# Which 48 expert tiles get their first product early: tiles 0 to 47, or 48 spread evenly over all 128

## The chip, the core and the metric

The kernel runs on one core of a Trainium2 chip. The metric is the device time of one execution in microseconds (us); for the kernel before it is the median of three runs. The profile is of one execution more, and its times count from the start of its span.

## What is computed

The reference is a decoder block: two gated token mixers, a memory attention, and an expert layer. The change lies in the expert layer, whose core is this:

```python
def chunk(args):                      # 128 tokens
    hc, ic, gc = args                 # states, 128 expert numbers and 128 gates per token
    a = jnp.einsum('cd,ced->ce', hc, u[ic])
    a = jax.nn.gelu(a, approximate=False) * gc.astype(hc.dtype)
    return jnp.einsum('ce,ced->cd', a, v[ic])
```

There are 1024 tokens of width 1024 and 16384 experts. Each token uses 128 of the experts, each a row of `u` and a row of `v`.

## The kernel before

The tokens are worked in two halves of four blocks of 128. The first half **gathers** its expert rows: GpSimd issues an indirect DMA for each expert slot (L1035 for `u`, L1051 for `v`, 512 of each, 0.5 MB apiece), and VectorE multiplies the rows (L1038 for `u`, L1057 for `v`). These steps are spread over the program by a pace: each piece of matmul work ticks a clock by its cost (`self.pace.tick`), and the next gather step comes when `u_each` us of ticks have passed. In the part that matters here `u_each` is 2.0. A gather lands in one of seven `rows` buffers, which VectorE frees.

The second half is **dense** (`dense`, L1192). It computes all 16384 experts for 512 tokens, as 128 expert tiles of 128 experts, and multiplies by a matrix of gates that is zero where a token doesn't use the expert.

- The *first product* of a tile (`first`, L1210): load a `u` tile (`uraw`, three buffers), split it into a high and a low part (ScalarE L112, VectorE L113, `uT`, two buffers), and run 24 matmuls into a PSUM tile `acc` (two buffers in the second part).
- Gelu (L1253), then the product with the gates (VectorE L1254, in the tile `wl`), then a split of the result (L112, L113) into `c`, seven buffers per half.
- The *second product* (`second`, L1260): four tiles make a group, 32 groups in all. Four `v` tiles are loaded (`vraw`) and split (`v`, four buffers), and 96 matmuls go into eight PSUM tiles, four of them kept over all groups (`kept`) and four (`out`, two buffers) added by VectorE into `accu` (L1283).

`dense` has two parts. In the **early part** the gate matrices `Wd` are built and stored to DRAM, while 48 tiles get their first product and gelu (L1223 to L1228); each result, 128x512 numbers, is stored to DRAM as `ga`. In the **second part** `group(gi + 1)` is issued ahead of `second(gi)`. For a tile in `ga`, `group` loads the stored result (L1250) into a tile `c` that has one buffer; for any other tile it runs the first product. So on TensorE the first products of a group come just ahead of the second product of the group before it. The gates are loaded for two tiles at a time (L1246, `wl`, two buffers). All loads and stores but the gathers go through SP's queue, in program order; a load that waits for its buffer holds back all that is behind it there. A scheduler sets the order on each engine from the dependences and its own estimates.

The few lines that decide which path a tile takes:

```python
if e in ga:
    c = sp.tile([P, DT], F32, name="c", bufs=1)
    nc.sync.dma_start(c, ga[e])
else:
    c = first(e)
    nc.scalar.activation(c, c, AF.Gelu)
nc.vector.tensor_tensor(w, c.rearrange("p (j n) -> p j n", j=2 * ND), w, op=OP.mult)
```

Of the kernel before, what the change touches and what calls it, by code (L numbers as in the profile page):

```python
# [84 lines left out]
class K:  # L85
# [1106 lines left out]
    def dense(self, psum, early):  # L1192
# [4 lines left out]
        NE = P  # L1197
        with ExitStack() as ctx:
# [11 lines left out]
            def first(e):  # L1210
                uT = load_u(e)
                o = self.acc()
                for k in range(KD):
                    self.mm3(o, [u[:, k] for u in uT], [x[:, k] for x in h3], k == 0, k == KD - 1)
                self.pace.tick(KD * 3 * 0.216)
                return o

            ga = {}
            with ExitStack() as c2:
                self.wb = c2.enter_context(self.pool("wb"))  # L1220
                self.u_each = U_EACH[-2]
                self.pace.add("weights", self.weights(blks))
                for e in range(early):  # L1223
                    o = first(e)
                    t = self.wb.tile([P, 512], F32, name="gelu", bufs=2)
                    nc.scalar.activation(t, o, AF.Gelu)
                    ga[e] = self.scratch([P, 512], f"ga{e}")
                    nc.sync.dma_start(ga[e], t)  # L1228
                self.pace.drain("weights")
# [201 lines left out]
```

## Time and profile before

| what | us |
|---|---|
| median of three runs | 3481.64 (3471.62 to 3495.5) |
| the profiled execution: its own time | 3480.88 |
| its span, from the first to the last instruction | 3479.1 |

The busy shares over the span are 87% on TensorE (PE), 82% on VectorE (DVE), 40% on ScalarE (ACT) and 40% on GpSimd (POOL). These are averages over stages with different limits, so the second part of `dense` is read by itself. A DMA share of 1.00 means that all 16 DMA engines had a packet in hand all the time. PEclk is the granted clock of TensorE: 1.00 is 2.4 GHz, 0.50 is 1.2 GHz, and what lies between is a mean of the two.

### The profile page before, as it was taken

Reading aid. Unit: us, or ns where it says so; the run is one execution under the profiler, and the core shown is the slowest. Engines: PE = TensorE matmul, PEld = TensorE weight load, DVE = VectorE, ACT = ScalarE, POOL = GpSimd, SP = SyncE. Lnnn points to the kernel's source line nnn. Section 1 sums busy time; section 2 is a strip of 40 time slices with the busy share of each in tenths; the row PEclk is TensorE's granted clock in tenths of the full one; section 3 lists DMA queues with packets and bytes.
Section 4 is the critical chain, followed back from the end, with each engine's and each line's share of the span. In section 5 each row is a group of like instructions: output and inputs, shape, how many; then the busy total and the mean of one; then the engine's idle time right before and its main releaser. Section 6 shows DMA issues by size and latency. Waiting matters only on the chain. (4 is left out here: it accounts for less than half of the span.)

```text
span 3479.1 us, 42293 instructions
## 1 busy us (share of the span) xinstructions
PE 3023.2 (87%) x13234; PEld 2293.0 (66%) x13234; DVE 2849.2 (82%) x6623; ACT 1404.7 (40%) x2537; POOL 1396.1 (40%) x1122
## 2 busy tenths in 40 slices
PE   8999888798788798777899897588899999999997
PEld 6778765553345675545777675466677887877886
DVE  6656544588969889888999899677799999999998
ACT  5756344345656451322455557222122222222222
POOL 0010000011245346554123566334456666676664
PEclk9999998899888799778999999799899999999999
DMA  4575444435699479888567999999999999999997
GB/s 139 164 183 139 164 140 138 134 121 182 197 299 317 139 246 366 308 319 299 167 222 272 381 384 389 360 303 309 312 348 375 379 378 357 368 384 379 382 376 269
DMA packets 394209, 964.64 MB, mean 277 GB/s; under 512 B 36712, under 2 KB 146048, under 8 KB 392576
## 3 DMA queue, kind: packets, MB, share of 16 engines
q0 software_dynamic: 155264, 560.01, 45.4%
q1 hardware_dynamic: 238720, 401.94, 33.7%
q8 instruction: 104, 1.70, 0.2%
q14 instruction: 121, 0.99, 0.1%
HBM read 871.64 MB, written 90.18 MB: 276 GB/s over the span
## 5 line engine op out<-in xcount | busy, mean ns | idle before, releaser
L1035 POOL DMA_INDIRECT rows<-in_peer_u_dram,ii x512 | 679.8, 1328 | 903.9 <-DVE rows L1038 284.2
L1051 POOL DMA_INDIRECT rows<-in_peer_v_dram,ii x512 | 652.9, 1275 | 419.8 <-DVE h3s L1057 269.0
L1057 DVE SCALAR_TENSOR_TENSOR h3s<-rows,wexp,h3s 128x1024 f32<-128x1024 f32 x508 | 650.8, 1281 | 34.9 <-DMA rows<-in_peer_v_dram,ii 26.0
L1038 DVE SCALAR_TENSOR_TENSOR rows<-rows,h3s 128x1024 f32<-128x1024 f32 x512 | 610.2, 1218 | 72.5 <-DMA rows<-in_peer_u_dram,ii 72.1
L135 PE MATMUL acc<-fT,uT 128*128 128x512 f32 x1024 | 417.0, 407 | 39.1 <-ACT uT L112 21.7
L137 PE MATMUL acc<-fT,uT 128*128 128x512 f32 x1024 | 410.1, 400 | 3.1 <-DVE uT L113 3.0
L136 PE MATMUL acc<-fT,uT 128*128 128x512 f32 x1024 | 409.8, 400 | 0.0
L112 ACT ACTIVATE c<-wl 128x512 fp32r<-128x512 f32 x128 | 80.0, 631 | 758.9 <-PE out L136 458.9
L149 POOL TENSOR_TENSOR rstd<-msq,mhalf 128x1 f32<-128x1 f32 (+1 forms) x42 | 34.4, 819 | 595.1 <-DVE msq L147 578.3
L135 PEld LDWEIGHTS acc<-fT,uT 128*128 128x128 f32 x1024 | 195.9, 191 | 85.2 <-ACT uT L112 22.1
L136 PE MATMUL kept<-v,c 128*128 128x512 f32 x512 | 206.1, 406 | 38.0 <-DVE v L113 37.9
L135 PE MATMUL kept<-v,c 128*128 128x512 f32 x512 | 201.7, 400 | 38.1 <-ACT v L112 38.1
L137 PEld LDWEIGHTS acc<-fT,uT 128*128 128x128 f32 x1024 | 195.4, 191 | 59.3 <-issue 12.3
L112 ACT ACTIVATE uT<-uraw 128x1024 fp32r<-128x1024 f32 x128 | 135.6, 1059 | 235.8 <-PE acc L136 162.0
L136 PEld LDWEIGHTS acc<-fT,uT 128*128 128x128 f32 x1024 | 195.9, 191 | 39.6 <-issue 0.7
L135 PE MATMUL out<-v,c 128*128 128x512 f32 x512 | 203.9, 398 | 9.3 <-DVE accu L1283 9.3
L113 DVE TENSOR_TENSOR w<-wraw,w 128x512 fp32r<-128x512 f32 (+1 forms) x176 | 116.4, 679 | 116.2 <-ACT w L112 109.2
L137 PE MATMUL kept<-v,c 128*128 128x512 f32 x512 | 204.3, 399 | 0.0
L136 PE MATMUL out<-v,c 128*128 128x512 f32 x512 | 203.5, 397 | 0.0
L137 PE MATMUL out<-v,c 128*128 128x512 f32 x512 | 203.3, 397 | 0.0
L568 ACT ACTIVATE junk<-W,xb 128x384 bf16<-128x384 f32 (+5 forms) x186 | 163.7, 880 | 78.4 <-DVE xb L566 75.6
L133 PE MATMUL acc<-wraw,hT 128*128 128x512 f32 (+1 forms) x384 | 168.7, 593 | 15.7 <-ACT tok L355 10.0
(361 smaller groups left out, 6710.7 us busy)
## 6 DMA issues: line engine op xcount, KB each, us to landing
uraw<-in_peer_ut_dram SPq DMA_DIRECT2D x128, 512.0 KB, 8.6
vraw<-in_peer_v_dram SPq DMA_DIRECT2D x128, 512.0 KB, 8.7
Wd<-wbuf SPq DMA_DIRECT2D x64, 512.0 KB, 9.1
wl<-Wd SPq DMA_DIRECT2D x64, 512.0 KB, 9.6
wraw<-in_w_in_dram SPq DMA_DIRECT2D x40, 512.0 KB, 3.7
fraw<-in_w_in_dram SPq DMA_DIRECT2D x32, 512.0 KB, 5.8
wraw<-in_w_out_dram SPq DMA_DIRECT2D x24, 512.0 KB, 3.7
ga<-gelu SPq DMA_DIRECT2D x48, 256.0 KB, 5.3
```

The lines of the kernel that those rows point to most:

```text
L112: self.nc.scalar.activation(hi, src, AF.Copy)
L113: self.last_dve = self.nc.vector.tensor_tensor(lo, src, hi.bitcast(F32), op=OP.subtract).ins
L133: self.last_pe = nc.tensor.matmul(out, l[0], r[0], start=start, stop=stop).ins
L135: nc.tensor.matmul(out, l[0], r[0], start=start, stop=False)
L136: nc.tensor.matmul(out, l[0], r[1], start=False, stop=False)
L137: self.last_pe = nc.tensor.matmul(out, l[1], r[0], start=False, stop=stop).ins
L149: nc.gpsimd.tensor_tensor(r, v, self.mhalf[:, :n], op=OP.pow)
L568: nc.scalar.activation(junk[:, :(b + 1) * P], self.W[b], AF.Sign, bias=xb[:, j:j + 1].bitcast(F32), accum_out=s[:, j:j + 1])
L1035: nc.gpsimd.indirect_dma_start(out=u, out_offset=None, in_=a["peer_u"][0], in_offset=bass.IndirectOffsetOnAxis(ap=ii[:, j:j + 1], axis=0))
L1038: nc.vector.scalar_tensor_tensor(u, u, 1.0, h3, op0=OP.mult, op1=OP.mult, accum_out=aa[:, j:j + 1])
L1051: nc.gpsimd.indirect_dma_start(out=v, out_offset=None, in_=a["peer_v"][0], in_offset=bass.IndirectOffsetOnAxis(ap=r["ii"][:, j:j + 1], axi ...
L1057: nc.vector.scalar_tensor_tensor(o, v, w[:, j:j + 1], o, op0=OP.mult, op1=OP.add)
```

## The change

```diff
-                for e in range(early):
+                for e in (e for e in range(NE) if (e + 1) * early // NE > e * early // NE):
```

With `early` 48 and `NE` 128 the early tiles were 0 to 47. They are now the tiles whose number modulo 8 is 2, 5 or 7. Before, groups 0 to 11 had four stored tiles each and groups 12 to 31 none. Now even groups have one stored tile and three first products, and odd groups have two of each. No instruction is added or taken away; the early part does the same number of first products on other tiles.

On SP's queue, at the start of the second part, there stood before (after the last store of `Wd`; `uraw` here are loads for later tiles):

```order
L1205 DMA uraw<-in_peer_ut_dram 128x1024 x2
L1246 DMA wl<-Wd 128x8x128
L1250 DMA c<-ga_13695 128x512
L1246 DMA wl<-Wd 128x8x128
L1265 DMA vraw<-in_peer_v_dram 128x1024 x2
L1250 DMA c<-ga_13780 128x512
L1265 DMA vraw<-in_peer_v_dram 128x1024 x2
L1250 DMA c<-ga_13853 128x512
L1265 DMA vraw<-in_peer_v_dram 128x1024
L1246 DMA wl<-Wd 128x8x128
L1250 DMA c<-ga_13954 128x512
```

And at the same place now:

```order
L1205 DMA uraw<-in_peer_ut_dram 128x1024 x2
L1246 DMA wl<-Wd 128x8x128 x2
L1250 DMA c<-ga_13695 128x512
L1265 DMA vraw<-in_peer_v_dram 128x1024 x3
L1246 DMA wl<-Wd 128x8x128
L1250 DMA c<-ga_13780 128x512
L1265 DMA vraw<-in_peer_v_dram 128x1024 x3
L1250 DMA c<-ga_13853 128x512
L1246 DMA wl<-Wd 128x8x128
L1205 DMA uraw<-in_peer_ut_dram 128x1024
```

The loads of `ga` stood one behind the other with few `v` loads between; now three of them stand among eight `v` loads and five `u` loads in each pair of groups. The `u` tiles of the first five first products (tiles 0, 1, 3, 4 and 6) are loaded ahead of the stores of `Wd`, as those of tiles 48 to 52 were before.

On VectorE, where one second product ends and the next begins, a group with four stored tiles read thus before (`wl` is the product with the gates, `c` and `v` are splits):

```order
L113 TENSOR_TENSOR c_19527<-wl,c_19526 128x512
L1254 TENSOR_TENSOR wl<-c,wl 128x8x64
L113 TENSOR_TENSOR v_19554<-vraw,v_19553 128x1024
L113 TENSOR_TENSOR c_19534<-wl,c_19533 128x512
L113 TENSOR_TENSOR v_19560<-vraw,v_19559 128x1024
L1254 TENSOR_TENSOR wl<-c,wl 128x8x64
L113 TENSOR_TENSOR v_19566<-vraw,v_19565 128x1024
L113 TENSOR_TENSOR c_19543<-wl,c_19542 128x512
L113 TENSOR_TENSOR v_19572<-vraw,v_19571 128x1024
```

Now, in a group with two stored tiles (`uT` is the split of a `u` tile, L1038 the product of a gathered row):

```order
L113 TENSOR_TENSOR c_20614<-wl,c_20613 128x512
L113 TENSOR_TENSOR v_20883<-vraw,v_20882 128x1024
L1283 TENSOR_TENSOR accu<-accu,out 128x512
L113 TENSOR_TENSOR v_20889<-vraw,v_20888 128x1024
L113 TENSOR_TENSOR v_20895<-vraw,v_20894 128x1024
L1254 TENSOR_TENSOR wl<-c,wl 128x8x64
L113 TENSOR_TENSOR v_20901<-vraw,v_20900 128x1024
L1038 SCALAR_TENSOR_TENSOR rows,aa<-rows,h3s 128x1024
L1254 TENSOR_TENSOR wl<-acc,wl 128x8x64
L113 TENSOR_TENSOR uT_21048<-uraw,uT_21047 128x1024
L113 TENSOR_TENSOR c_20820<-wl,c_20819 128x512
L113 TENSOR_TENSOR c_20827<-wl,c_20826 128x512
```

Between the four splits of `v` there were two products with stored tiles, each with its own load to wait for; now there is one. On TensorE the pattern of the second part was eleven second products in a row (1056 matmuls), a pair of first products (48), and then a second product (96) and four first products (96) in turn. It is now 96 and 72, 96 and 48 in turn, from five first products ahead of the first second product to the last two second products in a row.

## Rows read from the trace of the kernel before

**Rows 1.** Windows of the second part: length; busy by engine; PEclk; DMA share; GB/s.

```profile
core 0: us, PE busy (x) PEld busy (x) DVE busy (x) ACT busy (x) POOL busy (x), PEclk, DMA share, GB/s
2198.00:2225.00 27.00, 0.00 (x0) 0.00 (x0) 10.19 (x9) 1.47 (x2) 8.16 (x8) 0.50 1.02 381
2225.00:2545.00 320.00, 269.72 (x1051) 212.92 (x1052) 249.71 (x346) 73.13 (x98) 123.51 (x95) 0.90 0.91 309
2545.00:3437.00 892.00, 872.90 (x3792) 716.50 (x3791) 843.84 (x1020) 244.79 (x319) 590.30 (x435) 0.99 1.00 373
3437.00:3465.00 28.00, 23.60 (x103) 18.88 (x101) 26.68 (x29) 9.58 (x14) 9.74 (x7) 0.96 0.69 234
```

**Rows 2.** Timeline from 3455: TensorE's last matmul and the last store.

```profile
3460.22 0.39 PE L137 MATMUL out<-v,c 128*128 128x512 f32 x1
...
3475.52 0.33 SPq L1072 DMA_DIRECT2D out_dram<-rows  x1
```

**Rows 3.** Waits of SP's queue, 2225 to 2545: engine, line, releaser; total, times, longest.

```profile
SPq L1250 <- DMA c<-ga: 109.3, 37, 6.6
SPq L1250 <- DVE wl L1254: 66.4, 45, 7.0
```

**Rows 4.** Waits of VectorE, 2225 to 2545.

```profile
DVE wl L1254 <- DMA c<-ga: 34.1, 24, 4.0
DVE wl L1254 <- DMA wl<-Wd: 21.4, 5, 6.8
```

**Rows 5.** Waits of TensorE, 2225 to 2545.

```profile
PE kept L135 <- ACT v L112: 38.1, 2, 35.3
PE kept L136 <- DVE v L113: 37.9, 17, 4.8
```

**Rows 6.** Waits of TensorE (first row) and VectorE (second), 2600 to 3400.

```profile
PE acc L135 <- DVE wl L1254: 16.4, 8, 3.7
...
DVE rows L1038 <- DMA rows<-in_peer_u_dram,ii: 27.1, 21, 4.6
```

**Rows 7.** Windows of 100 us: one full of matmuls, and two of fast transfers.

```profile
2000.00:2100.00 100.00, 89.51 (x482) 70.40 (x480) 90.28 (x97) 60.39 (x75) 64.32 (x51) 0.98 1.00 388
2100.00:2200.00 100.00, 67.36 (x395) 52.52 (x394) 88.50 (x103) 59.48 (x76) 61.35 (x51) 0.90 1.00 387
...
2700.00:2800.00 100.00, 100.00 (x441) 82.46 (x440) 98.56 (x96) 24.85 (x32) 65.96 (x51) 1.00 1.01 381
```

**Rows 8.** Timeline at the start: first products of two tiles, loads, first second product.

```profile
2178.76 0.48 PE L135 MATMUL acc<-fT,uT 128*128 128x512 f32 x1
...
2190.71 0.58 ACT L1253 ACTIVATE acc<-acc 128x512 f32<-128x512 f32 x1
...
2198.43 1.28 SPq L1246 DMA_DIRECT2D wl<-Wd  x1
2204.72 1.46 SPq L1246 DMA_DIRECT2D wl<-Wd  x1
2220.99 0.69 DVE L1254 TENSOR_TENSOR wl<-c,wl 128x512 f32<-128x512 f32 x1 [10.00 <-DMA c<-ga]
2225.27 0.79 PE L135 MATMUL kept<-v,c 128*128 128x512 f32 x1 [35.33 <-ACT v L112]
```

**Rows 9.** Landing of the two `wl` loads of rows 8.

```profile
DMA to landing us min/median/max: 17.9/19.4/21.0
```

**Rows 10.** Timeline where a second product ends (PE) and the splits behind it (DVE).

```profile
2762.35 0.39 PE L137 MATMUL out<-v,c 128*128 128x512 f32 x1
...
2763.94 0.69 DVE L113 TENSOR_TENSOR c<-wl,c 128x512 fp32r<-128x512 f32 x1
2766.28 3.49 DVE L113 TENSOR_TENSOR v<-vraw,v 128x1024 fp32r<-128x1024 f32 x3
```

**Rows 11.** DMA issues: loads of `vraw`, 2210 to 2560 and 2560 to 3479; last number is landing.

```profile
vraw<-in_peer_v_dram SPq DMA_DIRECT2D x52, 512.0 KB, 5.7
...
vraw<-in_peer_v_dram SPq DMA_DIRECT2D x76, 512.0 KB, 10.2
```

## The prediction

> **What bounds the kernel now.** The change can act only in the second part of `dense`, so I read the windows first, cut where the matmul pattern changes [rows 1]. There are four stretches. From 2198 to 2225 TensorE does nothing. From 2225 to 2545 it runs eleven second products, 1056 matmuls in 320 us, and nothing on the chip is full: VectorE is busy 249.7 of 320 us (78%), the DMA engines 91%, and the clock is at 0.90 of full. From 2545 to 3437 the stretch with first products runs 3792 matmuls in 892 us; TensorE is busy 98%, VectorE 95% (843.8), DMA 100%, clock 0.99. The last second product and the final norms follow; the last matmul starts at 3460.2 and the last store at 3475.5 [rows 2].
>
> So one matmul costs 320 / 1056 = 0.303 us in the first stretch and 892 / 3792 = 0.2352 us in the second. Back to back it is 100 / 441 = 0.2268 us [rows 7]. The first stretch holds 320 - 1056 x 0.2268 = 80 us that TensorE doesn't need, the second 32 us.
>
> The waits say why. In the first stretch SP's queue stands 109.3 us because the load of `ga` needs the landing of the one before, and 66.4 us because its only buffer is still being read [rows 3]: 175.7 us over some 46 loads, 3.8 us each, with everything behind it held back. VectorE stands 34.1 us for `ga` and 21.4 us for the gates [rows 4], and as the splits of `v` are queued behind those products, TensorE stands for `v`: 17 waits of 2.2 us on VectorE's part, beside one of 35.3 us at the start [rows 5]. A second product with no first product ahead of it also has nothing to run while `v` is split. In the second stretch TensorE waits only 16.4 us in 800 for VectorE, and VectorE 27.1 us for gathered rows [rows 6].
>
> **The change, part by part.** The early part keeps its work: 48 tiles in the same places, and the stores the same. I cost it at nothing; TensorE and VectorE do there what they did.
>
> *The start.* Before, two first products (tiles 48 and 49) ran from 2178.8 and their gelus ended at 2191.3 [rows 8]; they then held both `acc` buffers. Now tiles 0 and 1 run there, and three more first products must come before the first second product. Their `u` tiles are loaded already, but `acc` comes free only when VectorE has multiplied tiles 0 and 1 with their gates. The gates are issued at 2198.4 and 2204.7 and land 17.9 to 21.0 us later [rows 8, 9], so at about 2219 and 2223. From 2219, two first products take 2 x 24 x 0.2268 = 10.9 us, some 3 us more at the half clock that the idle time leaves (0.50 in [rows 1]), and the third 5.4 us. The first second product starts at about 2240 where it was 2225.3 [rows 8]: 15 us late, with 72 matmuls more done. If the gates come late or the third `acc` waits for tile 3, it is 2260; if they land early, 2235.
>
> *The rest.* From there 4872 matmuls are left (6144 in all, less 48 x 24 and 5 x 24), 4776 without the last second product. Each group now has two or three first products, so the mixture is that of the second stretch with fewer of them. I take three sums, each by what the second stretch showed, and let the longest decide.
>
> - TensorE: 4776 x 0.2352 = 1123 us, so 2240 + 1123 = 3363.
> - VectorE: the work is the same. Its busy time over the four stretches is 10.2 + 249.7 + 843.8 + 26.7 = 1130.4 us [rows 1]. By 2240 some 22 are done (10.2, and 15 us at 78%), and 26.7 fall after the last second product has begun, so 1082 are left. At 843.84 / 892 = 0.946 that takes 1144 us: 3384.
> - DMA: bytes are conserved too. 381 x 27 + 309 x 320 + 373 x 892 + 234 x 28 gives 10.3 + 98.9 + 332.7 + 6.6 = 448.5 MB; 15 are moved by 2240 and 6.6 at the end, so 427 are left. At 373 GB/s that takes 1145 us: 3385.
>
> From the start of the last second product to the end of the span it took 3479.1 - 3437 = 42 us, which I keep. The longest sum ends at 3385 + 42 = 3427; the profiled execution took 1.8 us more than its span, and it lies 0.8 us under the median, so I make no other allowance. **That is 3428 us**, 53 less than 3480.9.
>
> The stall that goes is the `ga` chain. Three loads in eight tiles with about 73 us between their beginnings and ends (312 matmuls x 0.2352) leave the one buffer time, at 3.8 us each. Next in line is VectorE, whose work per group becomes even: its order now has 14 to 19 gathered rows between the splits of one group and the next, where it had 6 to 10 in most of the first stretch and 17 to 24 in the second.
>
> *The added tightness.* The four splits of `v` can only begin when a second product ends, and must be done when the next begins. Between them lay 96 matmuls, 21.8 us; now 72 or 48 do, 16.3 or 10.9 us. The splits ended 7.2 us after the last matmul (2762.6 to 2769.8) [rows 10], and one product with a stored tile is now among them. The cover is 3 us in a short gap. I cost it at nothing; the bounds are nothing and the 7.3 us that a group lost in the first stretch (320 / 11 = 29.1, less 96 x 0.2268 = 21.8).
>
> On the memory side the rows show 373 GB/s held over 892 us, and 388 and 387 over 100 us each [rows 1, 7]. The Trainium skill ("DMA: Bandwidth & Descriptors", Specifications) gives about 358 GB/s as what HBM yields to one core; by that the 427 MB would take 1193 us and the kernel would end at 3477, almost no gain. The trace stays above that figure, so the measurement decides, and the sum goes by 373.
>
> **Rivals.**
>
> *The DMA engines are the limit already, and their busy time is conserved.* For it: their share is 1.00 over the whole second stretch, and loads of `v` land in 10.2 us there against 5.7 in the first [rows 1, 11]. Then only the idle 9% of the first stretch can be won. The busy time is 27.5 + 291.2 + 892 + 19.3 = 1230 us; less 41 by 2240 and 19 at the end, 1170 are left, and the kernel ends at 2240 + 1170 + 42 = 3452, so 3454 us. Against it: a busy engine moved 340 GB/s in the first stretch (309 / 0.91) and up to 388 elsewhere, so busy time is not a fixed price per byte. The Trainium skill ("DMA: Bandwidth & Descriptors", Issuing engines are not separate DMA queues) says that all queues share the same 16 engines; that agrees with the landing times and is what this rival needs.
>
> *The chain of `ga` stays.* The single buffer and SP's order remain, and the loads now stand ahead of `u` and `v` loads that TensorE needs. If half of VectorE's 55.5 us of waits [rows 4] comes back on top of the sum, it is 3428 + 28 = 3456 us. Against it: the spacing above. This is the case in which the change doesn't do what it says.
>
> *The wait for `v` moves on and grows: slower.* Its place is the end of each second product, most of all the 16 short gaps. TensorE has 3437 - 2240 - 4776 x 0.2268 = 114 us to lose before the time is that of before, 3.7 us for each of 31 groups. If short gaps cost 7.3 us as the groups of the first stretch did, and the others half of it, the loss is 16 x 7.3 + 15 x 3.65 = 172 us: 2240 + 1083 + 172 + 42 = 3537, so 3539 us. For it: VectorE is nearly full, and gathered rows stand ahead of the splits in its order. Against it: in the second stretch the splits began 1.4 us after the last matmul with the same load.
>
> *TensorE alone decides.* If evening out lets VectorE and DMA run fuller, the first sum holds: 3363 + 42 + 2 = 3407 us, or somewhat less.
>
> **How the numbers follow.** Forecast 3428 (3410 to 3446): 0.55. DMA limit 3454: 0.17. `ga` chain 3456: 0.10. Slower, 3539: 0.08. TensorE alone, 3407 or less: 0.10. One per cent, about what a measurement of this kernel can tell from no change, is 35 us. Faster by more (under 3447) are nearly all of the forecast, the last case and a little of the DMA case: 0.66. Within it are most of the DMA case, the chain case, and small rests: 0.27. Slower by over 1%: 0.07. The range runs from 3395 to 3475: it takes in the start bounds and the DMA and chain cases, and leaves out the slower case and the far end of the last.
>
> **What would show it.** Right: no stretch with VectorE near 78%; over the whole second part matmuls at about 0.235 us, VectorE at 95%, DMA at 1.00 and 370 to 380 GB/s; SP's waits on `ga` down from 176 us to under 40; the first second product at about 2240; the last matmul near 3410. Wrong: waits of TensorE on the splits of `v` over 60 us in all, with PEclk falling below 0.95 (the slower case); DMA at 1.00 with TensorE and VectorE both waiting for landings (the DMA case); VectorE standing tens of us for `ga` (the chain); or a first second product after 2270.

## The result: slower by 3.9%, and the profile after

| what | before | after |
|---|---|---|
| median | 3487.05 us | 3623.36 us |
| single runs | 3471.62 to 3495.5 | 3601.48 to 3632.24 |
| span of the profiled execution | 3479.1 us | 3625.5 us |

The ratio is 1.0387, with a 95% interval of 1.0325 to 1.0449. The forecast was 3428 us, within 3395 to 3475: the sign is wrong.

The windows of the kernel after, cut at the first and near the last second product, answer to [rows 1] (same columns):

```profile
2198.00:2240.00 42.00, 18.81 (x72) 15.37 (x73) 24.89 (x27) 10.65 (x14) 10.13 (x9) 0.66 1.00 369
2240.00:3580.00 1340.00, 1157.53 (x4803) 933.69 (x4802) 1084.33 (x1353) 309.04 (x407) 697.92 (x526) 0.92 0.91 318
```

The work is what the prediction counted: 72 matmuls before 2240, and 1084.33 us of VectorE behind it, where 1082 had been worked out. But one matmul now takes 1340 / 4803 = 0.279 us, where 0.2352 was expected. VectorE is busy 81%, not 95%, the DMA engines 0.91 at 318 GB/s, and the clock is at 0.92. So the whole second part looks like the old first stretch, and by its busy share no engine is full.

The timeline of TensorE and of the stores shows the first second product, the last matmul and the last store:

```profile
2240.00 0.39 PE L135 MATMUL kept<-v,c 128*128 128x512 f32 x1
...
3595.83 0.39 PE L137 MATMUL out<-v,c 128*128 128x512 f32 x1
...
3621.87 0.33 SPq L1072 DMA_DIRECT2D out_dram<-rows  x1
```

The start comes at 2240, as forecast. The last matmul is at 3595.8 instead of about 3410, and 3460.2 before [rows 2]. From there to the last store it is 26.0 us, 15.3 before: 11 us are lost at the end, where VectorE still has gathered rows to add, and all the rest lies between.

The waits of VectorE from 2240 to 3580 answer to [rows 4] (engine, what was to run, releaser; total, times, longest):

```profile
DVE wl L1254 <- DMA wl<-Wd: 152.2, 33, 9.1
DVE wl L1254 <- issue: 52.6, 11, 6.6
DVE rows L1038 <- DMA rows<-in_peer_u_dram,ii: 24.5, 21, 2.6
DVE wl L1254 <- DMA vraw<-in_peer_v_dram: 15.0, 2, 7.8
```

The three rows on `wl` make 219.8 us. They are the products of L1254, and no row names `ga` any more: what VectorE now stands for is the load of the gates. The groups by line say that it is the 48 stored tiles alone. After:

```profile
L1254 DVE TENSOR_TENSOR wl<-c,wl 128x512 f32<-128x512 f32 x48 | 33.2, 692 | 219.7 <-DMA wl<-Wd 152.2 <-issue 52.6 <-DMA vraw<-in_peer_v_dram 15.0
L1254 DVE TENSOR_TENSOR wl<-acc,wl 128x512 f32<-128x512 f32 x80 | 54.6, 683 | 10.8 <-DMA wl<-Wd 9.6 <-ACT acc L1253 1.2
```

And before:

```profile
L1254 DVE TENSOR_TENSOR wl<-c,wl 128x512 f32<-128x512 f32 x48 | 33.1, 690 | 70.6 <-DMA c<-ga 44.1 <-DMA wl<-Wd 21.4 <-issue 5.1
```

Behind the last bar stands the idle time of VectorE just ahead of these products. It grew from 70.6 to 219.7 us, 4.6 us for each stored product.

The waits of TensorE in the same stretch answer to [rows 5]:

```profile
PE acc L135 <- DVE wl L1254: 135.2, 15, 13.6
PE kept L136 <- DVE v L113: 37.3, 17, 4.3
PE out L135 <- DVE accu L1283: 9.5, 9, 3.2
```

The wait for the splits of `v` is what it was (37.9 us before). New are 135.2 us (16.4 in the 800 us of [rows 6]) in which the next first product waits for `acc` to be read by VectorE, which is the engine that stands.

One such stand, in VectorE's timeline (start, duration; in brackets the idle time before it and what ended it):

```profile
2835.08 0.68 DVE L1283 TENSOR_TENSOR accu<-accu,out 128x512 f32<-128x512 f32 x1
2835.68 2.35 DVE L113 TENSOR_TENSOR v<-vraw,v 128x1024 fp32r<-128x1024 f32 x2
2844.56 0.69 DVE L1254 TENSOR_TENSOR wl<-c,wl 128x512 f32<-128x512 f32 x1 [6.53 <-DMA wl<-Wd]
2845.17 2.35 DVE L113 TENSOR_TENSOR v<-vraw,v 128x1024 fp32r<-128x1024 f32 x2
```

And the load that it stood for, in SP's timeline:

```profile
2834.00 0.38 SPq L1246 DMA_DIRECT2D wl<-Wd  x1
```

SP issues the gates at 2834.0, when a split has freed their buffer. VectorE has done two splits of `v` by 2838.0 and comes to the stored product, 4 us after the issue. The gates are there at 2844.5. The next two splits of `v` need nothing but VectorE, but they are behind the product, and the second product of TensorE waits 2.9 us for them. It is much the same everywhere: over the 46 stored products that waited, worked out in this way from the two timelines, VectorE is at the product 4.0 us after the latest issue of gates, and the product starts 8.9 us after it (medians).

SP's waits, which answer to [rows 3]:

```profile
SPq L1246 <- DVE c L113: 531.9, 58, 21.6
SPq L1250 <- DVE wl L1254: 264.0, 44, 9.3
```

The wait of `ga` for the landing of the one before is gone, but `ga` stands 264 us for its buffer and the gates 532 us for theirs, because VectorE lets go of both late. The wait with the gates is no measure of the loss: e5 below, the fastest, still has 410.7 us of it (2237 to 3382).

### The profile page after: what moved, and what is told of

The parts are those of the page before. It is cut to its first block, busy times and chain, and to the rows that moved or that the text cites. A ratio compares the mean times of both kernels' runs of the same rounds, so it can differ in the third digit from the quotient of the medians.

```text
span 3625.5 us, 42283 instructions
## 1 busy us (share of the span) xinstructions
PE 3050.6 (84%) x13234; PEld 2307.1 (64%) x13234; DVE 2851.4 (79%) x6623; ACT 1402.9 (39%) x2537; POOL 1380.9 (38%) x1122
## 4 chain that ended last, share of the span: by engine, by line
issue 27%; PE 23%; DVE 21%; DMA 13%; POOL 11%; ACT 4%; SPq 1%; POOLq 0%; DVEq 0%; ACTq 0%
POOL rows L1035 6%; POOL rows L1051 4%; DVE h3s L1057 4%; PE acc L135 3%; PE acc L136 3%; PE acc L137 3%; DMA wl<-Wd 3%; DMA rows<-in_peer_v_dram,ii 2%; DVE rows L1038 2%; DMA so<-pq 2%; PE po L727 2%; DMA fraw<-in_w_in_dram 2%; PE fill L133 1%; DMA rows<-in_peer_u_dram,ii 1%; DVE uT L113 1%
## 5 line engine op out<-in xcount | busy, mean ns | idle before, releaser
L1051 POOL DMA_INDIRECT rows<-in_peer_v_dram,ii x512 | 639.1, 1248 | 547.8 <-DVE h3s L1057 380.9
L1038 DVE SCALAR_TENSOR_TENSOR rows<-rows,h3s 128x1024 f32<-128x1024 f32 x512 | 610.2, 1218 | 62.6 <-DMA rows<-in_peer_u_dram,ii 60.7
L135 PE MATMUL acc<-fT,uT 128*128 128x512 f32 x1024 | 430.8, 421 | 185.7 <-DVE wl L1254 164.3
L137 PE MATMUL acc<-fT,uT 128*128 128x512 f32 x1024 | 421.1, 411 | 2.8 <-DVE uT L113 2.8
L136 PE MATMUL acc<-fT,uT 128*128 128x512 f32 x1024 | 421.5, 412 | 0.0
L135 PEld LDWEIGHTS acc<-fT,uT 128*128 128x128 f32 x1024 | 203.8, 199 | 236.1 <-DVE wl L1254 141.5
L137 PEld LDWEIGHTS acc<-fT,uT 128*128 128x128 f32 x1024 | 202.1, 197 | 64.1 <-DVE uT L113 11.5
L136 PE MATMUL kept<-v,c 128*128 128x512 f32 x512 | 203.2, 397 | 37.4 <-DVE v L113 37.3
L136 PEld LDWEIGHTS acc<-fT,uT 128*128 128x128 f32 x1024 | 203.7, 199 | 41.8 <-issue 0.8
L112 ACT ACTIVATE uT<-uraw 128x1024 fp32r<-128x1024 f32 x128 | 135.2, 1056 | 231.2 <-issue 110.4
L1254 DVE TENSOR_TENSOR wl<-c,wl 128x512 f32<-128x512 f32 x48 | 33.2, 692 | 219.7 <-DMA wl<-Wd 152.2
L137 PE MATMUL kept<-v,c 128*128 128x512 f32 x512 | 201.2, 393 | 0.0
L135 PE MATMUL kept<-v,c 128*128 128x512 f32 x512 | 199.5, 390 | 0.0
```

The costliest lines, as they stand in the source:

```text
L112: self.nc.scalar.activation(hi, src, AF.Copy)
L135: nc.tensor.matmul(out, l[0], r[0], start=start, stop=False)
L136: nc.tensor.matmul(out, l[0], r[1], start=False, stop=False)
L137: self.last_pe = nc.tensor.matmul(out, l[1], r[0], start=False, stop=stop).ins
L1038: nc.vector.scalar_tensor_tensor(u, u, 1.0, h3, op0=OP.mult, op1=OP.mult, accum_out=aa[:, j:j + 1])
L1051: nc.gpsimd.indirect_dma_start(out=v, out_offset=None, in_=a["peer_v"][0], in_offset=bass.IndirectOffsetOnAxis(ap=r["ii"][:, j:j + 1], axi ...
```

## The experiments

Three theories stood against each other.

- *Theory 1.* A stored product has no matmul to wait for, so the order puts it on VectorE close behind the issue of its gates. The load lands later than that, and VectorE, which works in order, stands, with splits and `acc` products behind it.
- *Theory 2.* The short gaps between second products (48 or 72 matmuls, not 96) leave no room for the splits of `v`.
- *Theory 3.* The one buffer of the stored result `c` holds back the loads.

Ratios are to the kernel before in the same batch (medians 3480.8 to 3483.7 us). All experiments start from the changed kernel, but for e6.

**e1: the stored product ordered behind a first-product tile's.** `issue_after` gives the scheduler one more order to keep: the product of a stored tile comes behind the last product of a tile with a first product. The gaps, the buffers and the loads are left alone.

```diff
-                    nc.vector.tensor_tensor(w, c.rearrange("p (j n) -> p j n", j=2 * ND), w, op=OP.mult)
+                    c = c.rearrange("p (j n) -> p j n", j=2 * ND)
+                    if e in ga:
+                        with self.tc.issue_after(self.last_m):
+                            nc.vector.tensor_tensor(w, c, w, op=OP.mult)
+                    else:
+                        self.last_m = nc.vector.tensor_tensor(w, c, w, op=OP.mult).ins
```

> The spread as changed, but the product of a stored tile with its gates (L1254) is ordered on VectorE behind the last product of a tile with a first product, so that it no longer stands among the splits of v, where it waits for the load of the gates. Theory 1 (VectorE stands for the gates: 220 us of waits at L1254 before stored products in the changed kernel): those waits fall under 60 us, TensorE's wait of 135 us for acc falls under 40, time 3410 to 3455 us. Theory 2 (the gaps of 48 and 72 matmuls are too short for the splits of v): nothing changes in the gaps, time 3580 to 3640. Theory 3 (the one buffer for the stored results and SP's order): the loads keep buffer and order, time 3570 to 3640.

Measured: 3499.83 us, ratio 1.0053 (1.0034 to 1.0072), so 124 us less than the changed kernel. That is above the 3410 to 3455 given for theory 1. The groups by line, first those with first products, then the stored ones:

```profile
L1259 DVE TENSOR_TENSOR wl<-acc,wl 128x512 f32<-128x512 f32 x80 | 54.5, 682 | 11.0 <-DMA wl<-Wd 9.7 <-ACT acc L1253 1.3
L1257 DVE TENSOR_TENSOR wl<-c,wl 128x512 f32<-128x512 f32 x48 | 32.8, 684 | 86.1 <-DMA c<-ga 86.1
```

No stored product waits for gates: VectorE now comes to it some 14 us after their issue (median, from the two timelines), not 4.0. What is left, 86.1 us, is a wait for `ga`, all 16 times at the second stored tile of an odd group. The gaps are as short as ever, so theory 2 does not explain the loss.

**e2: three buffers for the gates** (room for it comes from freeing two constant tiles).

```diff
-    w2 = sp.tile([P, 2 * ND, 2, P // 2], F32, name="wl", bufs=2)
+    w2 = sp.tile([P, 2 * ND, 2, P // 2], F32, name="wl", bufs=3)
```

> The spread as changed, with three buffers for the gates (wl) instead of two; room for it is made by giving back the mask and one gain tile, which are used only before the second part. The gates of a pair can then be issued a pair earlier. Theory 1: waits of VectorE at L1254 fall from 220 to under 80 us, time 3410 to 3460 us. Theory 2 (short gaps): time 3580 to 3640. Theory 3 (one buffer for the stored results): 3570 to 3640.

Measured: 3650.02 us, ratio 1.0493 (1.0451 to 1.0534): a miss. The stored products, by line:

```profile
L1255 DVE TENSOR_TENSOR wl<-c,wl 128x512 f32<-128x512 f32 x48 | 33.2, 691 | 239.0 <-DMA wl<-Wd 189.1 <-issue 49.4 <-DMA c<-ga 0.5
```

The third buffer hardly moves the product away from its load: VectorE is at it 4.8 us after the latest issue, and it starts 9.8 us after it (medians of those that waited, read off the timelines as above; 4.0 and 8.9 in the changed kernel). The distance from issue to use stays short of the landing, so one buffer more doesn't help. Why the loads land later here is open.

**e3: eight buffers for the split results** in place of seven (room for them made as in e2), so that a later split is never what holds the gates.

```diff
-    ch = [sp.tile([P, DT], F32R, name=f"c{j}", bufs=7) for j in range(2)]
+    ch = [sp.tile([P, DT], F32R, name=f"c{j}", bufs=8) for j in range(2)]
```

> The spread as changed, with eight buffers for each half of the split results (c) instead of seven, room made in the same way; the fourth split of a group no longer waits for the end of the second product ahead of it, so the gates of the second pair, which wait for that split to free their buffer, are issued earlier. Theory 1, with the late issue of the gates as its cause: waits at L1254 fall to under 110 us, time 3430 to 3520 us. If the waits come from the load's landing time alone, they stay near 220 and the time near 3610. Theories 2 and 3: 3570 to 3640.

Measured: 3616.14 us, ratio 1.0393 (1.0340 to 1.0446). The stored products stand 243.9 us, and of TensorE's waits the largest is now for `accu` (145.3 us from 2240 to 3580; for `acc` 31.8). The time is that of the changed kernel, with 24 us more of stand but 4.2 us of waits for gathered rows in place of 24.5: what VectorE loses costs about the same, whichever of TensorE's waits it shows up in.

**e4: whole groups stored, spread evenly.** Twelve groups with four stored tiles each, every second or third group; the other 20 have four first products. The gaps are 96 or none, as in the kernel before.

```diff
-  for e in (e for e in range(NE) if (e + 1) * early // NE > e * early // NE):
+  for e in (e for e in range(NE) if (e // 4 * 12 + 12) // 32 > e // 4 * 12 // 32):
```

> The 48 early tiles spread by whole groups: 12 groups of four stored tiles, evenly among the 32, and 20 groups with four first products. The gaps between second products are 0 or 96 matmuls, as in the kernel before; 48 stored products wait for gates as in both. Theory 1: VectorE's waits at L1254 between 70 us (before) and 220 us (after), time 3470 to 3560 us. Theory 2 (the gaps decide): the same gaps as before, time 3460 to 3500. Theory 3 (chain of the stored loads inside a group): as before, 3460 to 3500.

Measured: 3582.53 us, ratio 1.0296 (1.0244 to 1.0348). The stored products stand 159.5 us, 136.1 of it for gates:

```profile
L1254 DVE TENSOR_TENSOR wl<-c,wl 128x512 f32<-128x512 f32 x48 | 33.1, 689 | 159.5 <-DMA wl<-Wd 136.1 <-issue 15.8 <-DMA c<-ga 7.7
```

The same tile groups in another sequence are 3% slower than before, with the old gaps. That is against theory 2 again. The stand lies in the range that I had given for theory 1, the time above its 3470 to 3560: a microsecond of stand cost more than that range allowed. TensorE waits 66.9 us for the splits of `v` here (2240 to 3560), its longest wait; whether the stands make it or the gaps of none, e4 alone doesn't say.

**e5: e1 with two buffers for the stored result.**

```diff
-    c = sp.tile([P, DT], F32, name="c", bufs=1)
+    c = sp.tile([P, DT], F32, name="c", bufs=2)
```

> The kernel of e1_behind (each stored product ordered behind the last product of a first-product tile) with two buffers for the stored result c instead of one. In e1_behind VectorE still stood 86 us in 2300:3400 for the landing of c<-ga, 16 times, all of them second stored tiles of odd groups. If the single buffer is the whole remainder (theory 3 on top of theory 1), that wait falls under 25 us, TensorE's waits on wl and accu (77 us) fall to about half, and the time is 3500 less some 50 to 80 us: 3420 to 3450 us, below both kernels. If something else limits e1_behind (transfers: share .97 there), VectorE stands for rows or gates instead and the time stays at 3480 to 3505.

Measured: 3421.26 us (3412.64 to 3426.78), ratio 0.9813 (0.9781 to 0.9845), 1.9% faster than the kernel before. The stored products by line, and below them the window from 5 us behind the start of the first second product (2231.93) to the last matmul (3382.22):

```profile
L1257 DVE TENSOR_TENSOR wl<-c,wl 128x512 f32<-128x512 f32 x48 | 32.7, 680 | 0.0
```

```profile
2237.00:3382.00 1145.00, 1117.73 (x4850) 917.77 (x4849) 1092.28 (x1364) 315.25 (x412) 710.03 (x534) 0.99 1.01 374
```

In this order stored products never stand. VectorE is busy 1092.28 / 1145 = 95.4%, the DMA engines all the time at 374 GB/s, and a matmul takes 1145 / 4850 = 0.2361 us. The gaps are those of the changed kernel, so theory 2 falls here too. In VectorE's timeline the stored product sits behind an `acc` product:

```profile
2813.67 3.49 DVE L113 TENSOR_TENSOR v<-vraw,v 128x1024 fp32r<-128x1024 f32 x3
2817.08 2.60 DVE L1057 SCALAR_TENSOR_TENSOR h3s<-rows,wexp,h3s 128x1024 f32<-128x1024 f32 x2
2819.59 0.68 DVE L1259 TENSOR_TENSOR wl<-acc,wl 128x512 f32<-128x512 f32 x1
2820.20 0.68 DVE L1257 TENSOR_TENSOR wl<-c,wl 128x512 f32<-128x512 f32 x1
```

**e6: the kernel before with two buffers for the stored result** (the edit of e5 alone).

> The kernel before with two buffers for the stored result c. This tests the first claim of the prediction, that the chain of ga loads through one buffer (176 us of waits of SP's queue, 34 of VectorE in 2225:2545) is what makes the first stretch slow. If so, most of the 80 us that TensorE does not need there goes: 3410 to 3450 us. If the gates loads and the splits of v are what hold the first stretch (no first product to run while v is split), SP's wait on ga goes but the time stays within 1%: 3460 to 3490.

Measured: 3481.05 us, ratio 0.9987 (0.9971 to 1.0003). SP's waits from 2225 to 2545, against [rows 3]:

```profile
SPq L1250 <- DVE wl L1254: 58.3, 46, 7.8
SPq L1250 <- DMA c<-ga: 36.6, 14, 7.6
SPq L1246 <- DVE c L113: 114.7, 23, 13.0
```

The first two fall from 175.7 to 94.9 us and the time stays. But the third, the wait of the gates for their buffer, was 51.3 us and is now 114.7, and VectorE stands as long as ever. Its stored products in the same stretch, in the kernel before and in e6:

```profile
L1254 DVE TENSOR_TENSOR wl<-c,wl 128x512 f32<-128x512 f32 x47 | 32.4, 690 | 60.6 <-DMA c<-ga 34.1 <-DMA wl<-Wd 21.4 <-issue 5.1
L1254 DVE TENSOR_TENSOR wl<-c,wl 128x512 f32<-128x512 f32 x47 | 30.9, 689 | 60.9 <-DMA c<-ga 28.0 <-DMA wl<-Wd 23.7 <-issue 9.2
```

TensorE's wait on the splits of `v` stays too, 36.8 us in 17 waits. So freeing SP of most of the `ga` chain was worth nothing by itself. The stands of VectorE, which it left in place, e6 does not test.

**e7: the changed kernel with two buffers for the stored result.**

> The changed kernel with two buffers for the stored result c and nothing else, so the stored products stay where the scheduler put them. Theory 1 (VectorE stands for the landing of the gates because the stored product comes right behind their issue): VectorE's waits on wl stay above 150 us and the time between 3570 and 3640. Theory 3 (the one buffer of c is what made the changed kernel slow): 3450 to 3500 us.

Measured: 3621.31 us, ratio 1.0381 (1.0342 to 1.0421). Theory 3 alone falls; the stored products still wait for their gates:

```profile
L1254 DVE TENSOR_TENSOR wl<-c,wl 128x512 f32<-128x512 f32 x48 | 33.2, 693 | 211.4 <-DMA wl<-Wd 192.3 <-issue 19.1
```

The second buffer is worth 2 us here, which is within the spread, and 79 us behind the new order (3499.83 to 3421.26): with the order of e1 the product stands later, holds its one buffer longer, and the load for the next stored tile in the group comes late.

**e8: a dose.** As e5, but only the stored products of the odd groups are ordered; the 16 of the even groups stand where the scheduler puts them.

```diff
-                    if e in ga:
+                    if e in ga and e % 8 != 2:
```

(The edit also has an `elif e in ga:` branch, left out here, with the plain product for the others.)

> The kernel of e5_behind_two_c, but the 16 stored products of the even groups are left where the scheduler puts them (between the splits of v, as in the changed kernel); the 32 of the odd groups stay ordered. This is a dose between 3421 (no stored product stands for its gates) and 3621 (48 do, 211 us of waits of VectorE). Theory 1: those 16 stand for their gates, 75 us in all as in e7_after_two_c, or up to 142 as in e3_eight_c where they alone came that early, and the time rises by about 0.95 us for each us of wait: 3490 to 3555 us. If the odd groups with their two stored products were what cost, or the short gaps, it stays near 3421 to 3440.

Measured: 3494.44 us, ratio 1.0027 (1.0003 to 1.0051). The ordered ones (L1257) and the others (L1259):

```profile
L1257 DVE TENSOR_TENSOR wl<-c,wl 128x512 f32<-128x512 f32 x32 | 21.8, 680 | 0.0
L1259 DVE TENSOR_TENSOR wl<-c,wl 128x512 f32<-128x512 f32 x16 | 11.1, 692 | 79.1 <-DMA wl<-Wd 48.0 <-issue 31.2
```

Sixteen products stand 79.1 us, and the time is 73.2 us above e5. Together:

| kernel | stand of VectorE at stored products, us | median, us | above e5, us per us of stand |
|---|---|---|---|
| e5 | 0.0 | 3421.26 | |
| e8 | 79.1 | 3494.44 | 0.93 |
| e1 | 86.1 (for `ga`) | 3499.83 | 0.91 |
| e4 | 159.5 | 3582.53 | 1.01 |
| e7 | 211.4 | 3621.31 | 0.95 |
| after | 219.7 | 3623.36 | 0.92 |
| e2 | 239.0 | 3650.02 | 0.96 |
| e3 | 243.9 | 3616.14 | 0.80 |

In all spread versions a microsecond in which VectorE stands at a stored product costs 0.8 to 1.0 us, whatever it stands for. That is what one expects of an engine that must be busy 95% of the time. In the profiled executions the first second product starts at 2232 us in e5 and at 2238 to 2255 in the others, and that is in the last column; without it the column would run from 0.73 to 0.91 (an estimate, as starts and medians are of different executions).

## Why the prediction was wrong

*The start* was right: 2240, with 72 matmuls more done.

*The three sums* were right as sums of work, but not as a time. In e5, where VectorE doesn't stand at stored products, the rates came out: 0.2361 us per matmul (0.2352 taken), VectorE 95.4% (94.6%), 374 GB/s (373), and 3421 us in place of 3428. Part of that closeness is luck, as two misses of the sum partly cancel and the profiled execution, 3412.6 us, was the fastest of four. The last second product began there some 24 us sooner than the 3385 of the longest sum (3382.2 less 21.8 is 3360): 8 us because the first one began at 2232 and not at 2240, the rest because VectorE was through its work sooner (1077 us of work in 1128 us, where 1082 in 1144 had been reckoned). Behind that start 50 us followed, not the 42 that I kept. So evening out is worth about what was forecast, but the change as it was made doesn't get it.

*The step that failed* is the second sum, "VectorE: the work is the same … At 843.84 / 892 = 0.946 that takes 1144 us". The work was the same, the share was not: 0.81. The 0.946 came from a stretch with no stored product in it. The stored products brought their stands from the first stretch along and more than trebled them, and those 219.7 us had no term in the sum. With 1084 us of work they make 1304 of the 1340 us that the stretch took; the waits for gathered rows (24.5 us) are most of the rest. Of the 10.8 us of the other 80 products, 9.6 fall before 2240.

The warning stood in [rows 4]: 34.1 and 21.4 us of stands at the stored products, in a stretch where VectorE was idle for 70 of 320 us, so that they seemed to cost nothing. But 60.6 of these 70 us were the stands at stored products themselves (the row under e6). With 249.7 us of work they fill 310 of 320 us, 97%, just as 1304 of 1340 after: VectorE had hardly any time to spare there either. I read the first as the `ga` chain, which the spacing would end, and passed over the second. What would have shown it is the distance in the order from the issue of the gates to the product that uses them, held against a landing time. In the order of the changed kernel, printed ahead of the prediction, the product stands three splits of `v` (3.5 us in [rows 10]) and one addition (0.7) behind a split of `c`; if it is that split which frees the gates' buffer, as in the timeline above, the distance is some 4 us. Landing times were there too: loads of `v` took 5.7 us in the first stretch and 10.2 in the second [rows 11]. Less 4 us and times 48, that is an estimate of 82 or 298 us of stand; 219.7 were measured. The Trainium skill ("PSUM — Partial Sum Buffer", Engine vs sequencer instructions) says that VectorE's queue is strictly first in, first out; the stand of 6.5 us with two ready splits behind it agrees.

*"The stall that goes is the `ga` chain"* was wrong in the changed kernel: the wait for `ga` went, and the wait for the gates took its place and more. For the kernel before, e6 shortens SP's waits on `ga` by 81 us and the time doesn't change clear of its interval. What held the old first stretch is by the sum above the stands of VectorE as a whole, for `ga` and for gates, but no run takes them out of the kernel before, so that is not shown. Nor does a run isolate what it costs that a second product there had no first product beside it to run while `v` is split.

*The added tightness*, costed at nothing, was right: TensorE's wait for the splits of `v` is 37.3 us after and 0.6 in e5, with the same short gaps.

*The rivals.* "The wait for `v` moves on and grows: slower" had the right sign, but its size and its place were wrong. It reckoned 172 us of loss over matmuls back to back; by the same sum it was 251 (3595.8 less 21.8, 2240 and 1083), so 3623 us came out and not 3539. The mark that it named, over 60 us of TensorE's waits on `v`, didn't appear; the other, a clock below 0.95, did. The chain of `ga` doesn't decide in the changed kernel (e7), yet it was the next thing late as soon as the gates were cured (e1). The spacing that I held against it, 73 us for three loads, was an average over eight tiles: the two stored tiles of an odd group, 5 and 7, follow each other far closer. The DMA limit did not decide: e5 ends 33 us below the 3454 that it gave, and keeps 374 GB/s up for 1145 us. That is above the 358 GB/s which the Trainium skill ("DMA: Bandwidth & Descriptors", Specifications) gives for one core; here the measurement decides, as in the prediction.

*What stays open.* The order and the stand are shown, and that moving the product cures it. Why the scheduler expects the gates so early was not tried on the chip; its estimate of a load's landing is the likely place. The row "issue" among the releasers (52.6 us) names no releaser; that it is the same gates load is likely, since it went with the rest in e1.

## What to carry to other kernels

When work that waits only for loads is moved among other work, give it a term of its own: for each such instruction, the landing time in the *new* surroundings less the time from issue to use in the new order, and all of it lost on an engine that is near full. Don't carry the busy share of a stretch to another mix of instructions, and add an engine's stands to its work before you call the rest slack: in the old first stretch 60.6 of 70 idle us were stands. If a scheduler puts an instruction close behind its load, order it behind something that is sure to come later, and then look which buffer is next: here the order was worth 124 us, the second buffer alone 2 (within the spread), and both 202.

## What was not expected of the hardware

The load of the gates, 512 KB, took 10 us or so in full traffic (issued 2834.0, there at 2844.5; the DMA engines were at 0.98 in between, at 349 GB/s). In the kernel before, the median of such a load from 2225 to 2545, where the DMA engines were at 0.91, was 7.4 us (the row's last number):

```profile
wl<-Wd SPq DMA_DIRECT2D x23, 512.0 KB, 7.4
```

From 2545 to 3437, where they were at 1.00, it was 11.1 us. The bytes are the same; in these rows the load took longer where the DMA engines were busier. The mean share of a long stretch doesn't give the time by itself: after the change it is 0.91 again, and the stored products that waited started 8.9 us after the issue (median).
